# Inverse square roots in VectorE's small operations: one step of third order and one of second order in place of three steps of second order, in a decoder trunk of mixed heads

## The chip, the cores and the metric

The kernel runs on one core of a Trainium2 chip, in one launch. The metric is device microseconds of the core, the median of several executions. Of the core's engines, TensorE (PE) multiplies matrices, VectorE (DVE) and ScalarE (ACT) work element by element, GpSimd (POOL) prepares some tables and sums, and SyncE (SP) starts the transfers (DMA). Every engine works through a queue of its own, strictly in order, and waits at an instruction whose operands are not there yet.

## The reference, cut to what matters

One layer of a decoder trunk over 2048 tokens of width 1024, in float32. What matters here is where an inverse square root is taken:

```python
def rms_norm(x):
    return x * lax.rsqrt(jnp.mean(x * x, axis=-1, keepdims=True) + EPS)      # EPS = 1e-6

h = rms_norm(x) * (1 + sc1) + sh1
# h @ w_in, split into heads of three kinds of token mixers, each head 64 wide:
o_r = rms_norm(retention(...)) * silu(rg)     # 4 heads, fixed decay
o_h = rms_norm(hgrn2(...)) * silu(hg)         # 8 heads, gated decay
o_a = rms_norm(gla(...)) * silu(ag)           # 4 heads, gated decay
x = x + g1 * ((concat(o_r, o_h, o_a) * head_gain) @ w_out)
h = rms_norm(x) * (1 + sc2) + sh2
x = x + g2 * conv_ffn(h)                      # up (1024 to 2 x 2816), conv of 3 taps, silu gate, down
out = rms_norm(x) * final_gain
```

## The kernel before, in words

**Tiles and stages.** Tokens lie on the free axis in blocks of 512 (TB, four blocks), features on the 128 partitions. Every float32 product with a weight is made as three matmuls of rounded high and low halves (`split3`, L252 to L256: L254, L255, L256). So each operand needs its high half (a copy or activation on ScalarE) and its low half, the difference (on VectorE).

The program has these stages. `startup` (to about 60 us) loads the first block, takes its norm and begins the first projections. The token mixer goes block by block (to about 1240 us); within a block the units follow ORDER (L36): h0, h1, g, h2, h3, r0, r1, where an h or r unit is two heads and g is the four GLA heads. Then the MLP, by a scheme of seven products over halves (up and down stages, twice, to about 2480 us), and `last_product` with the final norm.

**A gated unit** (`gated`, L638 on) works through levels of a tree within chunks. At each level TensorE multiplies scores (`lvh` in PSUM, L664), VectorE scales queries and keys for the next level (L672 `qbh`, L674 `kh`) and puts the scores into the attention matrix (L683). TensorE's next level needs L672 and L674.

**A post** (`post`, L565 to L576) follows each unit's attention output `o` (128 tokens by 4 chunks by 2 heads of 64): squares on ScalarE, their sums over each head on VectorE (L571, `oms`, 128 x 8), the mean with EPS (L572), the inverse root `ors` (`newton`), then two products of 128 x 512: by the root (L575) and by the gate (L576). TensorE then transposes `o` (L582, `oT`), ScalarE and VectorE make its two halves (L585, L586), and the output projection uses them (`y`). There are 32 posts, eight to a block, since the GLA unit has two. A retention unit has its state updates (`S`, L892 and L894) and masks (L906) in the same queue.

**The other norms.** `rstd` (L330 to L351) takes the sums of squares of a block from TensorE and the root of 128 x 4, and TensorE spreads it again (`bc`, L347). Its input norm gives `xn` (L365), then `ha_k` for the eight k slices, high half on ScalarE (L369), low half on VectorE (L372). `startup` has such a norm (L431 to L439). `last_product` has two of 128 x 2 (L1456 to L1467, `msn`, `rsn`, `bcn`).

**The root.** `newton(x, y, n)` begins from an integer guess (L155, the bits of x times -0.5 plus a constant), and makes three Newton steps of three operations each: a = -0.5 y y (L158), a = a x (L159), y = (a + 1.5) y (L160). With the operation that makes the mean (L341, L433, L572 or L1460) that is 11 small operations, each on the result of the one before. It is called 45 times: once in `startup`, 10 times through `rstd`, 32 times in posts, twice in `last_product`.

**What sets the order.** TensorE's order is written by hand: steps are put on a `Clock` of due times, and the matmuls stand in the order in which the steps come due. In `startup` the orders of VectorE, ScalarE and SyncE are written by hand as well. After it a scheduler places the instructions of VectorE, ScalarE and SyncE, by when operands are ready in its own reckoning and by priorities: `tc.high_priority` with an offset puts work ahead (HOT 600, CHAIN 400). The roots in `rstd` have CHAIN, those in `last_product` HOT, those in `post` none; L672, L674 and L683 have CHAIN, the addition to the residual (L989) HOT.

Of the kernel before, what the change touches and what calls it, by code (L numbers as in the profile page):

```python
# [15 lines left out]
ALU = mybir.AluOpType  # L16
# [3 lines left out]
D = 1024  # L20
# [4 lines left out]
NCH = TB // P  # L25
# [5 lines left out]
EPS = 1e-6  # L31
# [73 lines left out]
def trunk(ctx, tc, xT, vecs, cvec, cst, rope, msk, wada, win, walow, wgla, wout, wup, wdown, out):  # L105
# [36 lines left out]
    V, S, G, T = nc.vector, nc.scalar, nc.gpsimd, nc.tensor  # L142
# [7 lines left out]
    ones = c_all[:, C_ONE:C_ONE + 1]  # L150
    nc.sync.dma_start(c_all[:], cst)

    def newton(x, y, n):

        V.tensor_scalar(y[:].bitcast(I32), x[:].bitcast(I32), -0.5, MAGIC, op0=ALU.mult, op1=ALU.add)  # L155
        a = small("nw", n)
        for _ in range(3):
            V.scalar_tensor_tensor(a[:], y[:], -0.5, y[:], op0=ALU.mult, op1=ALU.mult)  # L158
            V.tensor_tensor(a[:], a[:], x[:], op=ALU.mult)  # L159
            V.scalar_tensor_tensor(y[:], a[:], 1.5, y[:], op0=ALU.add, op1=ALU.mult)  # L160


    oml = p1.tile([P, 4], F32, tag="oml", name="oml")
# [5 lines left out]
    r = small("lbr", 4)  # L169
# [160 lines left out]
    def rstd(acc, name, bc, then, bank=None, gap=4.5):  # L330

        bank = bank or late_ps

        def first():
            p = bank("ss" + name)
            for c in range(NCH):
                T.transpose(p[:, c * P:(c + 1) * P], acc[:, c * P:(c + 1) * P], ident)
            x, r = small("ms" + name, NCH), small("rs" + name, NCH)
            with tc.high_priority(offset=CHAIN):
                V.tensor_reduce(x[:], p[:].rearrange("p (c d) -> p c d", c=NCH), axis=mybir.AxisListType.X, op=ALU.add)  # L340
                V.tensor_scalar(x[:], x[:], 1.0 / D, EPS, op0=ALU.mult, op1=ALU.add)  # L341
                newton(x, r, NCH)
            clock.at(gap, lambda: second(r))

        def second(r):
            p = bank("bc" + name)
            for c in range(NCH):  # L347
                T.transpose(p[:, c * P:(c + 1) * P], r[:, c:c + 1].to_broadcast([P, P]), ident)
            S.copy(bc, p[:])
            then()  # L350
        return first  # L351
# [37 lines left out]
    def startup():  # L389


        x, W, pending = [], {}, []
# [36 lines left out]
        ps = late_ps("ssn1_0")  # L429
        for c in range(NCH):  # L430
            T.matmul(ps[:, c:c + 1], acc[:, c * P:(c + 1) * P], ones, start=True, stop=True)  # L431
        ms, r = small("msn1_0", NCH), small("rsn1_0", NCH)
        V.tensor_scalar(ms[:], ps[:, 0:NCH], 1.0 / D, EPS, op0=ALU.mult, op1=ALU.add)  # L433
        newton(ms, r, NCH)
        cast("f")
        bc = bc1[0] = new_bc1(0)
        ps = late_ps("bcn1_0")
# [127 lines left out]
    def post(o, sg, name):  # L565

        o8 = o[:].rearrange("p c (h e) -> p (c h) e", e=64)
        sq = late("osq" + name)
        S.activation(sq[:], o[:].rearrange("p c e -> p (c e)"), AF.Square)
        ms = small("oms" + name)  # L570
        V.tensor_reduce(ms[:], sq[:].rearrange("p (a e) -> p a e", e=64), axis=mybir.AxisListType.X, op=ALU.add)  # L571
        V.tensor_scalar(ms[:], ms[:], 1.0 / 64, EPS, op0=ALU.mult, op1=ALU.add)  # L572
        rs = small("ors" + name)
        newton(ms, rs, 8)
        V.tensor_tensor(o8, o8, rs[:].unsqueeze(2).to_broadcast([P, 8, 64]), op=ALU.mult)  # L575
        V.tensor_tensor(o[:], o[:], sg[:], op=ALU.mult)  # L576

# [842 lines left out]
    def last_product(s, y, acc):  # L1420


        ops = last_operands(s)
        n = TB // 2

        def run(banks, ps, cols, cost):
            for k, (A, B) in enumerate(ops):
                for p, bank in zip(ps, banks):
                    sl = slice(p * P, (p + 1) * P)
                    split3(bank, [a[:, sl] for a in A], [x[:, cols] for x in B], k == 0, k == len(ops) - 1)  # L1430
                    adv(3 * cost)

        left = {}

        def add(bank, p, cols):
            with tc.high_priority(offset=HOT):
                V.scalar_tensor_tensor(y[1, p][:, cols], bank, G2[:, p:p + 1], y[1, p][:, cols], op0=ALU.mult,
                                       op1=ALU.add)
                if p < 3:
                    sumsq(acc, y[1, p], p, f"n3_{s}_1_", sl=cols, first=False)  # L1440
                else:
                    left[cols.start] = late(f"sqn3_{cols.start}")
                    S.activation(left[cols.start][:, cols], y[1, p][:, cols], AF.Square)
                gain(p, cols)

        def gain(m, cols):
            S.activation(y[1, m][:, cols], y[1, m][:, cols], AF.Copy, scale=vec[:, V_FG + m:V_FG + m + 1])

        def norm(t, banks):
            cols = slice(t * n, (t + 1) * n)  # L1450

            def first():
                p = banks(f"ssn3_{s}_1_{t}")
                for c in range(2):
                    for src in (acc, left[t * n]):
                        T.matmul(p[:, c:c + 1], src[:, t * n + c * P:t * n + (c + 1) * P], ones, start=src is acc,  # L1456
                                 stop=src is not acc)
                x, r = small(f"msn3_{t}", 2), small(f"rsn3_{t}", 2)
                with tc.high_priority(offset=HOT):
                    V.tensor_scalar(x[:], p[:, 0:2], 1.0 / D, EPS, op0=ALU.mult, op1=ALU.add)  # L1460
                    newton(x, r, 2)
                clock.at(4.0, lambda: second(r))

            def second(r):
                p = banks(f"bcn3_{s}_1_{t}")
                for c in range(2):
                    T.transpose(p[:, c * P:(c + 1) * P], r[:, c:c + 1].to_broadcast([P, P]), ident)  # L1467
                for i in range(KD // 2):
                    src = y["pair", i][:].rearrange("p (a n) -> p a n", a=2)[:, :, cols]
                    V.tensor_tensor(src, src, p[:, 0:n].unsqueeze(1).to_broadcast([P, 2, n]), op=ALU.mult)  # L1470
                    nc.sync.dma_start(out[2 * s + 1, :, 2 * i:2 * i + 2, cols], src)
                if t == 1:
                    done.add(("n3", 2 * s + 1))
            return first
        for m in range(4, KD):
            gain(m, slice(0, TB))
        whole = slice(0, TB)
        banks = [lev_ps(f"dL{p}") for p in range(2)]
        run([b[:] for b in banks], (0, 1), whole, M512)
        for p, b in enumerate(banks):  # L1480
            add(b[:], p, whole)
        for t, (one, bank) in enumerate(((late_ps, lev_ps), (acc_ps, late_ps))):
            cols = slice(t * n, (t + 1) * n)
            banks = [one(f"dL{t}_{p}") for p in range(2)]
            for p, b in enumerate(banks):
                run([b[:, 0:n]], (2 + p,), cols, M256)
                add(b[:, 0:n], 2 + p, cols)
            clock.at(2.6, norm(t, bank))
# [175 lines left out]
```

## Time and profile before

| | |
|---|---|
| median of 3 runs | 2523.25 us (2519.96 to 2526.4) |
| the profiled execution | 2519.96 us, its span 2518.2 us |
| PE busy | 2449.9 us, 97% |
| DVE busy | 1973.8 us, 78%, 3610 instructions |
| ACT busy | 1171.2 us, 47% |
| granted TensorE clock, mean | 0.993 |

The span goes from the first to the last instruction of the profiled execution. A row of the timeline reads: start, duration, engine, line, operation, output <- inputs, shapes, count, and in brackets how long the engine stood idle before it and what released it. A row of a list of waits reads: engine, waiting line <- releasing engine and line: us in total, times, longest. "L160" is line 160 of the kernel before.

### The profile page before, as it was taken

What the parts mean: (1) busy time and instruction counts of PE and PEld (TensorE: products, weight loads), DVE (VectorE), ACT (ScalarE), POOL (GpSimd) and SP (SyncE); (2) the same over time, 40 slices, a digit from 0 to 9 for tenths busy, and PEclk for the clock granted to TensorE, in tenths of its full rate; (3) what the DMA queues carried; (4) which work ended last, traced back from release to release, by engine and by line L of the source; (5) the groups of instructions that cost most, each with busy time, mean ns of one, the idle gap of its engine ahead of it and who ended that gap; (6) DMA issues with size and microseconds to landing.
All of it is one profiled execution on the core that took longest, in us unless ns stands there. A gap on an engine that the chain in (4) does not pass through costs nothing.

```text
span 2518.2 us, 35181 instructions
## 1 busy us (share of the span) xinstructions
PE 2449.9 (97%) x12173; PEld 2059.6 (82%) x12173; DVE 1973.8 (78%) x3610; ACT 1171.2 (47%) x1992; POOL 147.8 (6%) x278
## 2 busy tenths in 40 slices
PE   5999999999999999999999999999999999999998
PEld 4888878888888888888788888888878888888887
DVE  7987888878688785877698888787778877778565
ACT  4343434434444444434454544555445554555452
POOL 1000000000000000000000000000001100010000
PEclk9999999999999999999999999999999999999998
DMA  8853459865689647885554444587665444448663
GB/s 307 305 166 135 162 184 333 290 218 169 223 285 328 210 158 257 308 303 180 188 193 158 160 151 149 166 283 244 210 208 187 151 141 148 151 133 275 208 195 121
DMA packets 232499, 525.12 MB, mean 209 GB/s; under 512 B 24928, under 2 KB 28032, under 8 KB 232320
## 3 DMA queue, kind: packets, MB, share of 16 engines
q1 hardware_dynamic: 229120, 512.38, 61.1%
q0 software_dynamic: 3200, 10.49, 1.1%
q8 instruction: 96, 1.57, 0.3%
q14 instruction: 83, 0.68, 0.1%
HBM read 397.46 MB, written 125.30 MB: 208 GB/s over the span
## 4 chain that ended last, share of the span: by engine, by line
PE 47%; DVE 1%; DMA 1%; issue 1%; ACT 1%; DVEq 0%; POOL 0%; ACTq 0%; POOLq 0%
PE X L254 6%; PE X L255 6%; PE X L256 6%; PE dX L255 3%; PE dX L254 3%; PE dX L256 3%; PE Z L255 3%; PE Z L256 3%; PE Z L254 3%; PE dY L255 2%; PE dY L256 2%; PE dY L254 2%; PE Y L255 1%; PE Y L256 1%; PE Y L254 1%; DMA s<-sumsu 1%
## 5 line engine op out<-in xcount | busy, mean ns | idle before, releaser
L254 PE MATMUL X<-B,A 128*128 128x512 f32 x572 | 225.1, 393 | 4.4 <-ACT u L1358 2.3
L255 PE MATMUL X<-B,A 128*128 128x512 f32 x572 | 224.1, 392 | 0.0
L256 PE MATMUL X<-B,A 128*128 128x512 f32 x572 | 224.1, 392 | 0.0
L1058 DVE TENSOR_TENSOR dA<-rd,dA 128x512 fp32r<-128x512 f32 x154 | 106.1, 689 | 84.2 <-ACT dA L1057 83.9
L1057 ACT CAST dA<-rd 128x512 fp32r<-128x512 f32 x154 | 95.5, 620 | 131.1 <-PE dY L256 44.4
L1058 DVE TENSOR_TENSOR A<-s,A 128x512 fp32r<-128x512 f32 x176 | 120.7, 687 | 37.5 <-ACT A L1057 37.0
L1057 ACT CAST A<-s 128x512 fp32r<-128x512 f32 x176 | 108.5, 618 | 66.2 <-PE Z L256 45.2
L256 PE MATMUL dX<-dB,dA 128*128 128x512 f32 x352 | 137.0, 389 | 0.0
L255 PE MATMUL dX<-dB,dA 128*128 128x512 f32 x352 | 137.0, 389 | 0.0
L254 PE MATMUL dX<-dB,dA 128*128 128x512 f32 x352 | 137.0, 389 | 0.0
L254 PEld LDWEIGHTS X<-B,A 128*128 128x128 f32 x572 | 108.2, 189 | 29.2 <-ACT u L1358 4.5
L256 PEld LDWEIGHTS X<-B,A 128*128 128x128 f32 x572 | 108.2, 189 | 22.6
L255 PEld LDWEIGHTS X<-B,A 128*128 128x128 f32 x572 | 108.2, 189 | 22.2
L255 PE MATMUL Z<-B,A 128*128 128x512 f32 x308 | 119.9, 389 | 0.0
L254 PE MATMUL Z<-B,A 128*128 128x512 f32 x308 | 119.9, 389 | 0.0
L256 PE MATMUL Z<-B,A 128*128 128x512 f32 x308 | 119.9, 389 | 0.0
L1058 DVE TENSOR_TENSOR dB<-rb,dB 128x512 fp32r<-128x512 f32 x154 | 105.6, 687 | 9.7 <-ACT dB L1057 9.6
L1058 DVE TENSOR_TENSOR A<-r,A 128x512 fp32r<-128x512 f32 x130 | 89.4, 688 | 29.6 <-ACT A L1057 29.3
L664 PEld LDWEIGHTS lvh<-qbh,kh 128*128 128x128 f32 x768 | 100.6, 192 | 14.2 <-issue 6.4
L1057 ACT CAST A<-r 128x512 fp32r<-128x512 f32 x130 | 81.0, 623 | 62.4 <-PE Z L256 59.9
L664 PE MATMUL lvh<-qbh,kh 128*128 128x128 f32 x768 | 102.6, 277 | 5.0 <-DVE kh L674 3.8
L254 PE MATMUL psqkvgr<-hqkvgr,ha 128*128 128x512 f32 x256 | 106.2, 415 | 0.0
(479 smaller groups left out, 6993.4 us busy)
## 6 DMA issues: line engine op xcount, KB each, us to landing
gs<-yv SPq DMA_DIRECT2D x154, 256.0 KB, 3.0
rb<-gs SPq DMA_DIRECT2D x154, 256.0 KB, 3.9
r<-wup SPq DMA_DIRECT2D x140, 256.0 KB, 3.4
s<-sumsu SPq DMA_DIRECT2D x136, 256.0 KB, 3.0
wada<-wada SPq DMA_DIRECT2D x48, 512.0 KB, 6.1
rd<-sumsd SPq DMA_DIRECT2D x88, 256.0 KB, 3.8
rd<-wdown SPq DMA_DIRECT2D x66, 256.0 KB, 3.9
x<-xT SPq DMA_DIRECT2D x64, 256.0 KB, 5.9
```

The lines of the kernel that those rows point to most:

```text
L254: T.matmul(ps, lhs[0], rhs[0], start=first, stop=False, skip_group_check=more)
L255: T.matmul(ps, lhs[0], rhs[1], start=False, stop=False, skip_group_check=more)
L256: T.matmul(ps, lhs[1], rhs[0], start=False, stop=last, skip_group_check=more)
L664: T.matmul(ps[:, c * P:(c + 1) * P].rearrange("p (h n s) -> p h n s", h=2, s=s), kq[:, c * P:(c + 1) * P], rhs, start=True, stop=True)
L1057: S.copy(hi, src)
L1058: V.tensor_tensor(lo, src, hi, op=ALU.subtract)
```

## The change

The mean's operation moves into `newton`, which now takes what the mean is made of, and scales it by 1/2.25. The integer guess is made of the scaled mean. The first step is of third order, with four operations: a = -0.5 y y, a = a x, a = (a + 5/3) a, y = (a + 1.25) y. Its polynomial is two thirds of the usual third-order step, so that y leaves it with the factor of 1.5 of the scaled mean taken out again. The second is a Newton step with -1.125 in place of -0.5, since x is still scaled. That is 9 small operations instead of 11.

```diff
@@ -150,14 +150,17 @@
-    def newton(x, y, n):
-
+    def newton(x, y, n, mean, eps=EPS):
+
+        V.tensor_scalar(x[:], mean[0], mean[1] / 2.25, eps / 2.25, op0=ALU.mult, op1=ALU.add)
         V.tensor_scalar(y[:].bitcast(I32), x[:].bitcast(I32), -0.5, MAGIC, op0=ALU.mult, op1=ALU.add)
         a = small("nw", n)
-        for _ in range(3):
-            V.scalar_tensor_tensor(a[:], y[:], -0.5, y[:], op0=ALU.mult, op1=ALU.mult)
+        for step in (lambda: V.scalar_tensor_tensor(a[:], a[:], 5.0 / 3, a[:], op0=ALU.add, op1=ALU.mult), None):
+            V.scalar_tensor_tensor(a[:], y[:], -0.5 if step else -1.125, y[:], op0=ALU.mult, op1=ALU.mult)
             V.tensor_tensor(a[:], a[:], x[:], op=ALU.mult)
-            V.scalar_tensor_tensor(y[:], a[:], 1.5, y[:], op0=ALU.add, op1=ALU.mult)
+            if step:
+                step()
+            V.scalar_tensor_tensor(y[:], a[:], 1.25 if step else 1.5, y[:], op0=ALU.add, op1=ALU.mult)
@@ -338,8 +341,7 @@
-                V.tensor_scalar(x[:], x[:], 1.0 / D, EPS, op0=ALU.mult, op1=ALU.add)
-                newton(x, r, NCH)
+                newton(x, r, NCH, (x[:], 1.0 / D))
@@ -430,8 +432,7 @@
-        V.tensor_scalar(ms[:], ps[:, 0:NCH], 1.0 / D, EPS, op0=ALU.mult, op1=ALU.add)
-        newton(ms, r, NCH)
+        newton(ms, r, NCH, (ps[:, 0:NCH], 1.0 / D))
@@ -569,9 +570,8 @@
-        V.tensor_scalar(ms[:], ms[:], 1.0 / 64, EPS, op0=ALU.mult, op1=ALU.add)
-        newton(ms, rs, 8)
+        newton(ms, rs, 8, (ms[:], 1.0 / 64))
@@ -1457,8 +1457,7 @@
-                    V.tensor_scalar(x[:], p[:, 0:2], 1.0 / D, EPS, op0=ALU.mult, op1=ALU.add)
-                    newton(x, r, 2)
+                    newton(x, r, 2, (p[:, 0:2], 1.0 / D))
```

VectorE's program has 90 instructions fewer. TensorE's and GpSimd's orders are the same; ScalarE's and SyncE's have the same instructions, some in another order. In VectorE's, many instructions of the token mixer stand in another place. Three places follow, VectorE each time. A number behind a name counts units and blocks where it is small (`ha_5` is slice 5 of the next block's input, `orsh_3_0` the root of the fourth h unit) and is otherwise the allocator's own. Between the edit in `newton` and the one in `post` a line stands one to three further down after than before (L247 is L250, L365 is L367, L372 is L374, L571 is L572); from L575 on the numbers are the same again. The root's L158, L159, L160 before are L159, L160, L163 after, where L158 is the new third-order operation.

The first head unit of block 0, at its post. Before:

```order
L158 SCALAR_TENSOR_TENSOR nw<-orsh_0_0_1214 128x8
L683 COPY_PREDICATED ath_1_0_1241<-m_all,lvh_1_4_1293 128x128x4
L159 TENSOR_TENSOR nw<-nw,omsh_0_0_1211 128x8
L616 TENSOR_TENSOR yg_1145<-qg_1132,kg_989 128x512
L247 TENSOR_TENSOR lhfh_2_1443<-rhfh_2_1444,hhfh_2_1442 128x1024
L160 SCALAR_TENSOR_TENSOR orsh_0_0_1214<-nw,orsh_0_0_1214 128x8
L672 TENSOR_TENSOR qbh_1_823<-qbh_1_823,eh_1_721 128x64x8
L575 TENSOR_TENSOR oh_0_0_1195<-oh_0_0_1195,orsh_0_0_1214 128x512
L674 TENSOR_TENSOR kh_1_719<-kh_1_719,eh_1_721 128x32x8
L576 TENSOR_TENSOR oh_0_0_1195<-oh_0_0_1195,sgh_0_712 128x512
L683 COPY_PREDICATED ath_1_0_1241<-m_all,lvh_1_8_1324 128x64x8
```

After:

```order
L163 SCALAR_TENSOR_TENSOR orsh_0_0_1211<-nw,orsh_0_0_1211 128x8
L683 COPY_PREDICATED ath_1_0_1237<-m_all,lvh_1_4_1289 128x128x4
L575 TENSOR_TENSOR oh_0_0_1193<-oh_0_0_1193,orsh_0_0_1211 128x512
L250 TENSOR_TENSOR lhfh_2_1439<-rhfh_2_1440,hhfh_2_1438 128x1024
L576 TENSOR_TENSOR oh_0_0_1193<-oh_0_0_1193,sgh_0_710 128x512
L672 TENSOR_TENSOR qbh_1_821<-qbh_1_821,eh_1_719 128x64x8
L674 TENSOR_TENSOR kh_1_717<-kh_1_717,eh_1_719 128x32x8
L683 COPY_PREDICATED ath_1_0_1237<-m_all,lvh_1_8_1320 128x64x8
L616 TENSOR_TENSOR yg_1143<-qg_1130,kg_987 128x512
```

The products by the root and by the gate (L575, L576) stood behind L616, a weight split (L247) and L672, with L674 between the two. Now the first of them stands right behind L683, with the weight split (now L250) between the two; L616, L672 and L674 went behind both.

The end of block 0, where the next block's input slices `ha_4` to `ha_7` are made while the post of the fourth h unit (`omsh_3_0`, `orsh_3_0`) and the first retention state (`S`, L892, L894) are in the same queue. Before, first:

```order
L372 SCALAR_TENSOR_TENSOR ha_4_2685<-xn_4_2682,mod,ha_4_2685 128x512
L372 SCALAR_TENSOR_TENSOR ha_6_2697<-xn_6_2694,mod,ha_6_2697 128x512
L571 TENSOR_REDUCE omsh_3_0_2947<-osqh_3_0_2945 128x8
L892 COPY S_112<-ur_0_2979 64x64
L572 TENSOR_SCALAR omsh_3_0_2947<-omsh_3_0_2947 128x8
```

and eleven rows further on:

```order
L894 SCALAR_TENSOR_TENSOR S_112<-S_112,c_all,ur_0_2979 64x64
L159 TENSOR_TENSOR nw<-nw,omsh_3_0_2947 128x8
L894 SCALAR_TENSOR_TENSOR S_112<-S_112,c_all,ur_0_2979 64x64
L160 SCALAR_TENSOR_TENSOR orsh_3_0_2950<-nw,orsh_3_0_2950 128x8
L372 SCALAR_TENSOR_TENSOR ha_5_2691<-xn_5_2688,mod,ha_5_2691 128x512
L372 SCALAR_TENSOR_TENSOR ha_7_2703<-xn_7_2700,mod,ha_7_2703 128x512
L158 SCALAR_TENSOR_TENSOR nw<-orsh_3_0_2950 128x8
```

After:

```order
L374 SCALAR_TENSOR_TENSOR ha_4_2671<-xn_4_2668,mod,ha_4_2671 128x512
L374 SCALAR_TENSOR_TENSOR ha_5_2677<-xn_5_2674,mod,ha_5_2677 128x512
L374 SCALAR_TENSOR_TENSOR ha_6_2683<-xn_6_2680,mod,ha_6_2683 128x512
L572 TENSOR_REDUCE omsh_3_0_2933<-osqh_3_0_2931 128x8
L892 COPY S_112<-ur_0_2963 64x64
L155 TENSOR_SCALAR omsh_3_0_2933<-omsh_3_0_2933 128x8
L892 COPY S_112<-ur_0_2963 64x64
```

and eight rows further on:

```order
L894 SCALAR_TENSOR_TENSOR S_112<-S_112,c_all,ur_0_2963 64x64
L163 SCALAR_TENSOR_TENSOR orsh_3_0_2935<-nw,orsh_3_0_2935 128x8
L894 SCALAR_TENSOR_TENSOR S_112<-S_112,c_all,ur_0_2963 64x64
L374 SCALAR_TENSOR_TENSOR ha_7_2689<-xn_7_2686,mod,ha_7_2689 128x512
L159 SCALAR_TENSOR_TENSOR nw<-orsh_3_0_2935 128x8
```

The low half of `ha_5` stood with that of `ha_7`, behind the second step of the root, and now stands between those of `ha_4` and `ha_6`, ahead of the sums of squares of the post; `ha_7` stands after the first step.

The end of block 3, at the post of the first retention unit (`or_0`), with the masks of the second (`atr_1`, L906), a residual addition (L989) and the low halves of an input of the MLP (`lB_6_1`, `lB_6_2`, L1058). Before:

```order
L159 TENSOR_TENSOR nw<-nw,omsr_0_11247 128x8
L1058 TENSOR_TENSOR lB_6_2_11435<-hm_6_2_11432,hB_6_2_11434 128x512
L160 SCALAR_TENSOR_TENSOR orsr_0_11250<-nw,orsr_0_11250 128x8
L906 TENSOR_TENSOR atr_1_11328<-scr_1_1_11333,c_all 128x512
L575 TENSOR_TENSOR or_0_11243<-or_0_11243,orsr_0_11250 128x512
L989 SCALAR_TENSOR_TENSOR x_3_6_11304<-y_0_7_11321,mod,x_3_6_11304 128x512
L576 TENSOR_TENSOR or_0_11243<-or_0_11243,sgr_0_10395 128x512
L586 SCALAR_TENSOR_TENSOR oTr_0_11365<-oTr_0_11360,vec,oTr_0_11365 128x512
```

After:

```order
L1058 TENSOR_TENSOR lB_6_1_11351<-hm_6_1_11348,hB_6_1_11350 128x512
L163 SCALAR_TENSOR_TENSOR orsr_0_11175<-nw,orsr_0_11175 128x8
L906 TENSOR_TENSOR atr_1_11252<-scr_1_0_11253,c_all 128x512
L575 TENSOR_TENSOR or_0_11169<-or_0_11169,orsr_0_11175 128x512
L906 TENSOR_TENSOR atr_1_11252<-scr_1_1_11257,c_all 128x512
L576 TENSOR_TENSOR or_0_11169<-or_0_11169,sgr_0_10325 128x512
L989 SCALAR_TENSOR_TENSOR x_3_6_11228<-y_0_7_11245,mod,x_3_6_11228 128x512
L1058 TENSOR_TENSOR lB_6_2_11357<-hm_6_2_11354,hB_6_2_11356 128x512
L586 SCALAR_TENSOR_TENSOR oTr_0_11289<-oTr_0_11284,vec,oTr_0_11289 128x512
```

L989 stood between the two products and `lB_6_2` ahead of both; both now stand behind the second product, and one L906 went in between the two.

## The prediction, made blind

> **What bounds the kernel now.** I read the page first (busy shares), then the busy time by stage, then TensorE's list of waits, and last the timeline around each wait that names a root. First the page's line of engines, and the row of the MLP's up stage from the busy times by stage (columns: the stretch and its length, PE, PEld, DVE, ACT and POOL busy with their counts, granted clock, DMA share, GB/s).
>
> ```profile
> PE 2449.9 (97%) x12173; PEld 2059.6 (82%) x12173; DVE 1973.8 (78%) x3610; ACT 1171.2 (47%) x1992; POOL 147.8 (6%) x278
> ...
> 1240.00:1650.00 410.00, 408.49 (x1799) 337.25 (x1798) 350.36 (x453) 215.21 (x321) 30.98 (x85) 1.00 0.49 161
> ```
>
> TensorE is the bound: it is idle for 2518.2 - 2449.9 = 68 us in all, and in the MLP's up stage for 410.00 - 408.49 = 1.5 us. VectorE is busy for 78%, but its busy time is not the path. A shorter root is worth something only where TensorE waits for it, and those places are in the next list (TensorE's waits: total us, times, longest).
>
> ```profile
> PE bcn L1467 <- DVE rsn L160: 4.6, 2, 2.7
> ...
> PE lvh L664 <- DVE kh L674: 3.8, 2, 3.4
> ...
> PE pshfh L255 <- DVE ha L372: 2.6, 1, 2.6
> ...
> PE oTh L582 <- DVE oh L576: 1.4, 2, 0.7
> ```
>
> The first row ends in a root itself (two of them, in the last stage); a third such wait, at the start, comes in the next fence. The last row ends in the product behind a head's root (L576). The two in the middle end in other work that stood behind a root in VectorE's queue. All other roots have no such wait, or one that is shown below; their saving stays in VectorE's slack.
>
> **Part 1: two operations fewer in a root that TensorE waits for.** The removed operations are of the kind of these rows (count, busy, mean ns), and the root at the start shows their spacing:
>
> ```profile
> L158 DVE SCALAR_TENSOR_TENSOR nw<-orsh 128x8 f32<-128x8 f32 x48 | 7.9, 164 | 0.4
> ...
> 18.57 0.16 DVE L159 TENSOR_TENSOR nw<-nw,msn 128x4 f32<-128x4 f32 x1
> 18.77 0.16 DVE L160 SCALAR_TENSOR_TENSOR rsn<-nw,rsn 128x4 f32<-128x4 f32 x1
> ...
> 18.98 1.11 PE L439 MATMUL bcn<-c_all,rsn 128*128 128x128 f32 x4 [2.23 <-DVE rsn L160]
> ```
>
> One operation is busy for 0.16 us, but the next one of a dependent chain starts 18.77 - 18.57 = 0.20 us after it. The four forms that the new root uses are of the same size and kinds as the old ones, so I price them alike. Two operations fewer on the path are 2 x 0.195 = **0.39 us** at the start, where VectorE goes from the root straight into the work that TensorE needs next. At the end it is the same twice (the 4.6 us of the list). The last root stands alone in the queue. In the one before it three operations follow the last large one of the queue, from here on:
>
> ```profile
> 2503.75 0.16 DVE L158 SCALAR_TENSOR_TENSOR nw<-rsn 128x2 f32<-128x2 f32 x1
> ```
>
> In the new order only one does. Sum 2 x 0.39 = **0.78 us**. Nothing late takes its place: what follows (the scaling and the last stores) waits for these two transposes.
>
> [...] The row of 164 ns agrees with the duration, not with the worth: on the path the step is 0.20, and between independent operations only 0.08 (next fence, 124.85 to 124.93).
>
> **Part 2: what the shorter root moves.** The order of VectorE changes in many places, because a root that needs fewer turns lets the scheduler place the products behind it earlier. First place, the first head unit of block 0 (the order before and after is shown above):
>
> ```profile
> 123.12 0.68 DVE L616 TENSOR_TENSOR yg<-qg,kg 128x512 f32<-128x512 f32 x1
> 123.72 1.21 DVE L247 TENSOR_TENSOR lhfh<-rhfh,hhfh 128x1024 fp32r<-128x1024 f32 x1
> 124.85 0.15 DVE L160 SCALAR_TENSOR_TENSOR orsh<-nw,orsh 128x8 f32<-128x8 f32 x1
> 124.93 0.68 DVE L672 TENSOR_TENSOR qbh<-qbh,eh 128x512 f32<-128x512 f32 x1
> 125.53 0.68 DVE L575 TENSOR_TENSOR oh<-oh,orsh 128x512 f32<-128x512 f32 x1
> 126.14 0.41 DVE L674 TENSOR_TENSOR kh<-kh,eh 128x256 f32<-128x256 f32 x1
> 126.47 0.68 DVE L576 TENSOR_TENSOR oh<-oh,sgh 128x512 f32<-128x512 f32 x1
> ...
> 127.29 0.63 PE L582 MATMUL oTh<-c_all,oh 128*128 128x128 f32 x4 [0.72 <-DVE oh L576]
> ...
> 128.46 1.06 PE L664 MATMUL lvh<-qbh,kh 128*128 128x128 f32 x8
> ...
> 166.87 0.63 PE L582 MATMUL oTh<-c_all,oh 128*128 128x128 f32 x4 [0.67 <-DVE oh L576]
> ```
>
> L616, L672 and L674 go behind L576. By their steps that is 0.60 + 0.60 + 0.33 = 1.53 us, and two small operations at 0.08 come to 0.16. L576 would end 1.7 us earlier, more than the 0.72 that TensorE waits. In exchange L672 starts about 0.5 us later and L674 about where it was, and the level's matmul at 128.46 comes 128.46 - 126.55 = 1.9 us after L674's end, so it has room. The same move is made in the next unit (row of 166.87). Sum 0.72 + 0.67 = **1.39 us**.
>
> Second place, the end of block 0:
>
> ```profile
> 295.21 1.41 DVE L372 SCALAR_TENSOR_TENSOR ha<-xn,mod,ha 128x512 fp32r<-128x512 f32 x2
> ...
> 301.16 1.41 DVE L372 SCALAR_TENSOR_TENSOR ha<-xn,mod,ha 128x512 fp32r<-128x512 f32 x2
> ...
> 301.96 0.50 PE L255 MATMUL pshfh<-ha,hhfh 128*128 128x512 f32 x1 [2.59 <-DVE ha L372]
> ```
>
> TensorE waits at its k = 5 for the low half of `ha_5`, the first of the two L372 at 301.16. It stands behind a root and the state updates between its operations. In the new order it stands directly behind `ha_4`, so it would be done at about 295.21 + 2 x 0.67 = 296.6, five us before it is needed. What is late next is `ha_7`: about 302, when TensorE is through with k = 5, its scores and k = 6. I take the whole **2.59 us**; the bounds are 0 (if `ha_7` takes the wait over) and 2.59.
>
> Then two retention roots lie in a stretch that VectorE works through almost without a pause until TensorE's long wait at 338:
>
> ```profile
> 337.93 2.04 PE L664 MATMUL lvh<-qbh,kh 128*128 128x128 f32 x8 [3.38 <-DVE kh L674]
> ```
>
> Four operations fewer at 0.20 are **0.80 us** out of these 3.38; at the 0.08 of interleaved ones they would be 0.32. I take the upper value, since the last operations of both roots stand without a filler.
>
> Third place, the end of block 3:
>
> ```profile
> 1190.89 0.68 DVE L575 TENSOR_TENSOR or<-or,orsr 128x512 f32<-128x512 f32 x1
> ...
> 1192.15 0.68 DVE L576 TENSOR_TENSOR or<-or,sgr 128x512 f32<-128x512 f32 x1
> ...
> 1192.98 0.63 PE L582 MATMUL oTr<-c_all,or 128*128 128x128 f32 x4 [1.21 <-DVE or L576]
> ...
> 1195.17 0.79 PE L596 MATMUL or<-S,qnr 128*128 128x128 f32 x2 [1.56 <-DVE oTr L586]
> ...
> 1237.98 0.50 PE L254 MATMUL X<-B,A 128*128 128x512 f32 x1 [1.99 <-ACT u L1354]
> ```
>
> In the new order L989 and L1058's `lB_6_2` go from ahead of L576 to behind it. The turns of two such operations, L575 and L989, take 1192.15 - 1190.89 = 1.26 us here. L576 would end about that much earlier, so the wait of 1.21 goes. But up to the MLP's first product TensorE also waits for transfers and for ScalarE (1.99 at 1237.98), and a gain can stand there. I take half of 1.21, **0.60 us**, with 0 and 1.21 as ends.
>
> Sum: 0.39 + 1.39 + 2.59 + 0.80 + 0.60 + 0.78 = **6.55 us**. The profiled execution took 2519.96 us (span 2518.2 and 1.76 around it) and would take 2513.4. It was the fastest of the three runs shown; against their median of 2523.25 the forecast is **2516.7 us**, 0.26% less. About 0.3%, or 7.6 us, is what a measurement of this kernel can tell from no change, so I call this case "same". With the unsure terms at their ends it gains 2.6 to 7.2 us.
>
> **Rivals.**
>
> *The clock goes up as well.* Two rows of busy times by stretch, the number ahead of the last two being the granted clock:
>
> ```profile
> 301.00:304.00 3.00, 2.04 (x9) 1.80 (x10) 2.83 (x9) 0.03 (x1) 0.00 (x0) 1.00 0.00 0
> ...
> 1195.20:1204.00 8.80, 8.80 (x33) 8.03 (x34) 2.48 (x9) 1.38 (x2) 0.18 (x3) 0.50 0.26 104
> ```
>
> After the waits of 1.21 and 1.56 us TensorE had half its clock for 8.8 us (1195.20 to 1204.00), which costs 4.4 us of its time; after the single wait of 2.59 at 302 the clock stayed at 1.00. If one wait of 1.56 is left, the half clock may not come. Then all 1.21 count (0.61 more) and 4.4 on top: -11.6 us, 2511.7. Against it stands that at other places a shorter idle stretch might meet the throttle instead, and that these rows do not tell when it strikes. [...]
>
> *The gains are taken back.* What TensorE gains before 1237 (5.77 us of the sum) is waited away where it next stands for a transfer or ScalarE, the 1.99 at 1237.98 growing by as much. Left are the two roots at the end, -0.8 us, 2522.5; if half is taken back, about -4. For it speaks that the list of waits has such places; against it that TensorE has only some 1.5 us of idle time in the whole stage behind it, so the transfers there have room.
>
> *Slower: the products of the heads stand in front of the levels.* A post has L575 and L576 (0.60 each), and the new order puts them ahead of level work in the queue of a strictly ordered engine. There are 32 posts. If each delays a level's L672 by the 0.5 us worked out for the first, and the level's matmul has less room than that, the price is 32 x 0.5 = 16 us, less 6.55: +9.5, 2532.7. It decides where the room is under 0.5 us; the one worked out above has 1.9, and before the change the level waits for kh come to 3.8 us in two places of the whole program.
>
> That the change does not do what it says is excluded: the order of VectorE has 90 small operations fewer, two in each of 45 roots.
>
> **How the numbers follow.** Forecast 0.40, the clock as well 0.34, taken back 0.17, slower 0.09. Faster by over 0.3%: the clock case and a little of the forecast whose terms all come at their upper ends, 0.36. Same: the rest of the forecast and the case taken back, 0.55. Slower 0.09. The range goes from the clock case with two us below it (a wait of the list that goes unasked) to the case taken back with two and a half above: 2510 to 2525. It leaves out the slower case and the outer ends.
>
> **What would show it.** In the changed profile: no wait for L372 at about 302 (if one of similar size stands at k = 7, that term fails); no waits before the transposes near 127 and 167; the wait at 338 shorter by 0.8; the waits of the list's first row 3.8 instead of 4.6; the granted clock around 1195 to 1204, which tells the forecast from the first rival; and the wait near 1238, which tells it from the second. New waits of the level matmuls (L664) for their operands in many places would make the prediction wrong.

## The result, and the profile after

The changed kernel takes 2512.49 us (median of 10 executions, 2505.55 to 2518.38) against 2523.56 us of the kernel before (10 executions, the three shown above among them). The ratio is 0.9958, with a 95% interval of 0.9945 to 0.9970: 11 us, or 0.42%, faster. The forecast was 2516.7, the first rival (the clock goes up as well) 2511.7.

The page's line of engines after:

```profile
PE 2442.4 (98%) x12173; PEld 2056.2 (82%) x12173; DVE 1962.9 (78%) x3520; ACT 1171.2 (47%) x1992; POOL 146.4 (6%) x278
```

The span of this execution is 2503.8 us, 14.4 less than before. TensorE's share of it splits in two. Its idle time fell from 68.3 to 2503.8 - 2442.4 = 61.4 us, so 6.9 us of waits went. Its busy time fell by 2449.9 - 2442.4 = 7.5 us, although it runs the same 12173 matmuls: that is the clock, 0.993 on average in the profile of before and 0.996 here. The profiled execution is the fastest of the ten, so its 14.4 us flatter the change.

TensorE's list of waits after, two of its rows:

```profile
PE lvh L664 <- DVE kh L674: 4.0, 3, 3.4
...
PE bcn L1466 <- DVE rsn L163: 3.8, 2, 2.3
```

The waits for the two last roots went from 4.6 to 3.8 us, as predicted. The rows of before for `oTh` on `oh` (1.4) and for `pshfh` on `ha` at the end of block 0 (2.6) are gone; the level's wait (3.8 before) is still there.

The timeline of TensorE at the places of the prediction, in the order of the program:

```profile
18.30 0.69 PE L440 MATMUL bcn<-c_all,rsn 128*128 128x128 f32 x2 [1.84 <-DVE rsn L163]
...
125.32 0.60 PE L582 MATMUL oTh<-c_all,oh 128*128 128x128 f32 x4
...
164.11 0.60 PE L582 MATMUL oTh<-c_all,oh 128*128 128x128 f32 x4
...
296.70 0.39 PE L258 MATMUL pshfh<-ha,hhfh 128*128 128x512 f32 x1
...
327.43 1.15 PE L664 MATMUL lvh<-qbh,kh 128*128 128x128 f32 x8 [0.38 <-DVE doth L645]
...
331.95 1.85 PE L664 MATMUL lvh<-qbh,kh 128*128 128x128 f32 x8 [3.38 <-DVE kh L674]
...
1182.57 0.60 PE L582 MATMUL oTr<-c_all,or 128*128 128x128 f32 x4
...
1184.73 0.49 PE L596 MATMUL or<-S,qnr 128*128 128x128 f32 x2 [1.56 <-DVE oTr L586]
...
1222.59 0.50 PE L257 MATMUL X<-B,A 128*128 128x512 f32 x1 [1.48 <-ACT u L1354]
...
1231.40 0.51 PE L257 MATMUL X<-B,A 128*128 128x512 f32 x1 [2.55 <-ACT u L1358]
...
2490.36 0.43 PE L1466 MATMUL bcn<-c_all,rsn 128*128 128x128 f32 x2 [1.48 <-DVE rsn L163]
...
2496.75 0.48 PE L1466 MATMUL bcn<-c_all,rsn 128*128 128x128 f32 x1 [2.29 <-DVE rsn L163]
```

A matmul without a bracket did not wait. The four waits in front of the transposes near 127, 167 and 1193 and in front of the matmul at 302 are gone. The wait of 1.56 us at the end of block 3 is still there. Two waits at the MLP's beginning read 1.48 and 2.55 us; before they were 1.99 and 0.77. The level's wait of 3.38 us has not moved, but the one ahead of it, 0.38 us here, was longer before:

```profile
333.40 1.15 PE L664 MATMUL lvh<-qbh,kh 128*128 128x128 f32 x8 [1.00 <-DVE doth L645]
```

VectorE at the first of those places, and the three low halves at the end of block 0:

```profile
121.36 0.72 DVE L683 COPY_PREDICATED ath<-m_all,lvh 128x512 f32<-128x512 uint32 x1
121.98 0.68 DVE L575 TENSOR_TENSOR oh<-oh,orsh 128x512 f32<-128x512 f32 x1
...
123.70 0.69 DVE L576 TENSOR_TENSOR oh<-oh,sgh 128x512 f32<-128x512 f32 x1
124.30 0.69 DVE L672 TENSOR_TENSOR qbh<-qbh,eh 128x512 f32<-128x512 f32 x1
...
292.90 2.07 DVE L374 SCALAR_TENSOR_TENSOR ha<-xn,mod,ha 128x512 fp32r<-128x512 f32 x3
```

L576 starts at 123.70 instead of 126.47. VectorE was 1.07 us ahead by then (its L683 stood at 122.43 and stands at 121.36), so the new order made L576 1.7 us earlier, the figure that was worked out. The low halves of slices 4 to 6 are one group that ends at 294.97. The one of slice 5, the middle one, ends a step of 0.66 us earlier, at about 294.3, so 2.4 us before the matmul of k = 5. The one of slice 7 stands alone, from 298.92 to 299.66, and its matmul starts at 299.82.

Last, the clock at the end of block 3 (busy times by stretch, the clock third from the end):

```profile
1184.80:1193.60 8.80, 8.80 (x51) 7.74 (x52) 4.42 (x14) 3.22 (x4) 1.43 (x6) 1.00 0.67 230
```

The 8.8 us at half clock that followed these waits before are gone here: in as long a time TensorE does 51 matmuls instead of 33.

### The profile page after: what moved, and what is told of

It is laid out like the page before. It is cut to its first block, busy times and chain, and to the rows that moved or that the text cites. A ratio compares the mean times of both kernels' runs of the same rounds, so it can differ in the third digit from the quotient of the medians.

```text
span 2503.8 us, 35090 instructions
## 1 busy us (share of the span) xinstructions
PE 2442.4 (98%) x12173; PEld 2056.2 (82%) x12173; DVE 1962.9 (78%) x3520; ACT 1171.2 (47%) x1992; POOL 146.4 (6%) x278
## 4 chain that ended last, share of the span: by engine, by line
PE 48%; DVE 1%; DMA 1%; issue 1%; ACT 0%; DVEq 0%; POOL 0%; ACTq 0%; POOLq 0%
PE X L257 6%; PE X L258 6%; PE X L259 6%; PE dX L257 3%; PE dX L259 3%; PE dX L258 3%; PE Z L257 3%; PE Z L258 3%; PE Z L259 3%; PE dY L257 2%; PE dY L259 2%; PE dY L258 2%; PE Y L257 1%; PE Y L258 1%; PE Y L259 1%
## 5 line engine op out<-in xcount | busy, mean ns | idle before, releaser
L1058 DVE TENSOR_TENSOR dA<-rd,dA 128x512 fp32r<-128x512 f32 x154 | 106.1, 690 | 87.1 <-ACT dA L1057 86.9
L1058 DVE TENSOR_TENSOR A<-s,A 128x512 fp32r<-128x512 f32 x176 | 120.7, 686 | 36.3 <-ACT A L1057 35.8
L1058 DVE TENSOR_TENSOR A<-r,A 128x512 fp32r<-128x512 f32 x130 | 89.4, 688 | 30.4 <-ACT A L1057 30.2
L1058 DVE TENSOR_TENSOR dB<-rb,dB 128x512 fp32r<-128x512 f32 x154 | 105.7, 687 | 8.9 <-ACT dB L1057 8.9
```

Of the source, the lines that this page charges most:

```text
L1058: V.tensor_tensor(lo, src, hi, op=ALU.subtract)
```

## The experiments

The ratio sets each run against the kernel before on the same chip. Beside it I use a second reading. Every execution carries its mean granted clock c, so that span x (1 - c) is, at most, what the reduced clock cost it, and span x c is the rest. Over 76 executions of before, taken beside the runs e1 to e12 on two chips, c is 0.9927 on average and the rest 2502.6 us, and every row is set against these. The executions of before in the first comparison have no clock on record, but for the profiled one. Half-clock stretches fall differently from execution to execution (at the end of block 3 for 10.2 us in the first profile of before, for 3.4 in that of e1), so the rest tells more finely what the waits did. Standard errors of the rest are 0.7 to 1.1 us (2.0 for the new root in all posts).

| kernel | ratio, 95% interval | mean clock | rest against before, us |
|---|---|---|---|
| the change, first 10 executions | 0.9958 (0.9945 to 0.9970) | 0.9945 | -5.8 |
| the change again (e8) | 0.9957 (0.9941 to 0.9973) | 0.9935 | -8.4 |
| before again (e1) | 0.9996 (0.9986 to 1.0007) | 0.9927 | -0.5 |
| old roots, posts ahead (e2) | 1.0011 (0.9998 to 1.0025) | 0.9915 | 0.0 |
| new roots and fillers (e3) | 0.9980 (0.9970 to 0.9991) | 0.9926 | -5.7 |
| all 32 posts (e4) | 0.9958 (0.9946 to 0.9970) | 0.9936 | -7.3 |
| last two posts (e5) | 0.9985 (0.9973 to 0.9998) | 0.9931 | -2.1 |
| the other 30 posts (e6) | 0.9975 (0.9965 to 0.9985) | 0.9931 | -5.1 |
| start and last norms (e7) | 0.9994 (0.9981 to 1.0007) | 0.9924 | -1.2 |
| first block's eight posts (e9) | 0.9971 (0.9960 to 0.9982) | 0.9935 | -4.5 |
| ten block norms (e10) | 0.9998 (0.9988 to 1.0008) | 0.9923 | -1.6 |
| one third-order step only (e11) | 0.9938 (0.9922 to 0.9953) | 0.9943 | -10.9 |
| roots of 13 operations (e12) | 1.0049 (1.0037 to 1.0062) | 0.9916 | +10.3 |

The theory: the change is worth the waits that a root, or something behind it in VectorE's queue, ends. The first rival: every removed VectorE operation is worth its time, 10.9 us over 90 = 0.12 us. The second: the gain is the clock.

**Before once more (e1)**, without an edit.

> The kernel before once more, under a name of its own, so that each of its executions shows its granted clock. Theory (the new order of VectorE takes waits of TensorE away): ratio 1.000 within 0.2%; a granted clock between 0.990 and 0.996 that changes from execution to execution, and times that go down by about 2.5 us for each 0.001 of it. Rival (the clock: before always meets a half clock near 1195 that the changed kernel always misses): the clock stays at 0.992 to 0.994 in every execution, below all of the changed kernel's.

The ratio is 1 within the interval. The clock of the single executions runs from 0.991 to 0.994, so half clocks come and go without any change. The clock alone doesn't tell the two kernels apart by execution either: the changed kernel's first ten run from 0.992 to 0.996. In the profile of e1 TensorE has half its clock behind the wait for `ha_5` at the end of block 0, where the first profile of before kept the full clock. The row of the wait, and the busy times behind it:

```profile
303.23 0.50 PE L255 MATMUL pshfh<-ha,hhfh 128*128 128x512 f32 x1 [2.68 <-DVE ha L372]
```

```profile
304.20:307.70 3.50, 3.50 (x10) 2.74 (x10) 2.79 (x5) 0.00 (x0) 0.56 (x2) 0.51 0.00 0
```

**Old roots, the posts' VectorE work ahead (e2).** The body of `post` from L570 on is put under a priority:

```diff
+        with tc.high_priority(offset=CHAIN):
             ms = small("oms" + name)
             ...
             V.tensor_tensor(o[:], o[:], sg[:], op=ALU.mult)
```

> Roots of 11 operations as before; only the priority of the VectorE work of the 32 posts is raised by 400, which moves it ahead in the first unit's post and brings the low half of slice 5 forward at the end of block 0, as in the changed kernel, but leaves the end of block 3 as it was. Theory of the order: the waits near 127, 167 and 302 go without any operation removed, -4 to -5 us (ratio 0.998). Rival (VectorE's time: each removed operation is worth its 0.12 us to TensorE): no operation is removed, so 0 us. Third view (levels delayed by posts that go ahead): +5 us or more.

As for the first block the theory held: TensorE's waits near 127, 167 and 302 are gone without a removed operation, and it is 4.5 us ahead at 302, 0.5 of them from the start already. But the run as a whole is not faster, since other waits have come. Two rows of its list of waits:

```profile
PE og L597 <- DVE S L714: 4.7, 2, 3.3
...
PE bcn L348 <- DVE rsn L160: 2.8, 2, 2.1
```

The second is a block norm's root. It shares its turns with a post's root in the kernel before too, without a wait. Here it ends 1.15 us earlier than there, but TensorE comes over 3 us earlier and waits 2.10 for it, so a part of the gain is waited away. The first row is shown by the timelines at that place. The kernel before comes first (SPq is SyncE's queue; L942 starts the two loads of a weight that L948 and the three operations behind it add up, and L948 needs the second of them):

```profile
1064.69 1.54 SPq L942 DMA_DIRECT2D wsu<-wup  x2
...
1073.14 0.69 DVE L948 TENSOR_TENSOR wsu<-wsu 128x512 f32<-128x512 f32 x1 [2.47 <-DMA wsu<-wup]
...
1077.91 3.67 DVE L713 SCALAR_TENSOR_TENSOR S<-S,eg,ug 32x64 f32<-32x64 f32 x12 [1.89 <-PE ug L703]
```

Then e2, where these lines are L943, L949 and L714:

```profile
1066.48 0.33 SPq L943 DMA_DIRECT2D wsu<-wup  x1
...
1070.18 0.32 SPq L310 DMA_DIRECT2D lvgh<-keptt_3l  x1
1073.27 0.38 SPq L302 DMA_DIRECT2D rqkvgr<-win  x1
1073.70 0.47 SPq L943 DMA_DIRECT2D wsu<-wup  x1
...
1081.76 0.69 DVE L949 TENSOR_TENSOR wsu<-wsu 128x512 f32<-128x512 f32 x1 [10.22 <-DMA wsu<-wup]
1082.37 2.71 DVE L714 SCALAR_TENSOR_TENSOR S<-S,eg,ug 32x64 f32<-32x64 f32 x9
...
1084.92 0.46 PE L597 MATMUL og<-S,qbg 128*128 128x128 f32 x2 [3.27 <-DVE S L714]
```

The busy times of e2 behind that wait:

```profile
1086.30:1093.00 6.70, 6.70 (x24) 5.83 (x24) 6.14 (x18) 2.26 (x3) 1.04 (x2) 0.50 0.31 116
```

A sum over the MLP's weights stands ahead of the state updates of the GLA unit in both kernels. What changed is SyncE's order: both loads of the sum are started together before, and in e2 the second stands behind two other loads, so that it starts some 8 us later. The sum (L949) waits 10.22 us for it, the states wait behind the sum, TensorE waits 3.27 us for them and has half its clock for 6.7 us after it. So an earlier post is no gain by itself. What else moves decides, in SyncE's queue too, and my expectation of -4 to -5 us was wrong.

**New roots and two idle operations (e3).** In the loop of the new `newton`:

```diff
+            d = small("nd", n)
+            V.tensor_tensor(d[:], x[:], x[:], op=ALU.mult)
```

> The changed kernel's roots of 9 operations, with two more small multiplications per root into a tile that nobody reads, so that VectorE has as many instructions as before. Theory of the order: the products still come early, most of the gain stays, -6 to -9 us (ratio 0.997), with the waits near 127, 167 and 302 gone; at the start and the end up to 0.4 us per root is lost. Rival (VectorE's time): the instructions are back, 0 us.

The product `d` is read by nobody. VectorE has as many instructions as before, and the kernel still gains: ratio 0.9980, the rest -5.7 us. That speaks against the price per operation. It does not speak against a price per busy time, because VectorE's busy time is 1966.8 us in this profile, 7.0 below before, although the count is the same. The kernel gains less than expected, and the profile shows one reason: the same sum (here L950) waits for its second load, which starts at 1070.39 behind the same two others, 7 us after the first at 1063.17.

```profile
1078.44 0.69 DVE L950 TENSOR_TENSOR wsu<-wsu 128x512 f32<-128x512 f32 x1 [10.21 <-DMA wsu<-wup]
...
1081.60 0.46 PE L598 MATMUL og<-S,qbg 128*128 128x128 f32 x2 [3.50 <-DVE S L715]
```

In the changed kernel the two loads are started together, as before (at 1058.08), and TensorE does not wait there.

**The new root in all posts alone (e4):** the new `newton` is called in `post` only.

> The new root in the 32 posts alone; start, block norms and last norms keep 11 operations. Theory of the order: all but the 0.39 at the start and 0.78 at the end, -9 to -10 us (ratio 0.9962). Rival (VectorE's time): 64 of 90 operations, -7.7 us. Rival of the sum as predicted: -6.55 + 1.17 = -5.4 us, the rest being the clock.

The posts carry nearly all: ratio 0.9958, the rest -7.3 us. The rival's -7.7 us, a ratio of 0.9969, lies inside the interval as well, so this run does not tell the two apart.

**The last two posts, and the other thirty (e5, e6).** `post` counts its calls:

```diff
+        posts.append(name)
+        if len(posts) > 30:          # e6: len(posts) <= 30
+            newton3(ms, rs, 8, (ms[:], 1.0 / 64))
+        else:
             V.tensor_scalar(ms[:], ms[:], 1.0 / 64, EPS, op0=ALU.mult, op1=ALU.add)
             newton(ms, rs, 8)
```

> The new root in two posts alone, those of the last block's two retention units; the order of VectorE changes only at the end of block 3, there as in the changed kernel. The wait of 1.21 us near 1193 goes in any case. Theory A (the half clock near 1195 came of that wait together with the one of 1.56 behind it): the mean granted clock rises from 0.993 to about 0.995 and the time falls by 4 to 6 us (ratio 0.998). Theory B (the half clock comes by chance and with all waits): the clock stays at 0.993, -1.2 us at most (ratio 0.9995), less if the MLP's waits take it back.

> The new root in the other 30 posts; the end of block 3, the start, the block norms and the last norms stay as before. Theory A (of the run before this one): the clock stays at 0.993, and the time falls by the waits alone, -5 to -6 us (ratio 0.9978). Theory B: the clock rises as far as in the changed kernel, to 0.994 to 0.995, and the time falls by 8 to 9 us (ratio 0.9966).

TensorE's timelines at the end of block 3, first of e5, then of e6, each with its clock behind it:

```profile
1195.60 0.60 PE L600 MATMUL oTr<-c_all,or 128*128 128x128 f32 x4
```

```profile
1196.10:1204.90 8.80, 7.24 (x45) 6.36 (x44) 4.49 (x14) 2.37 (x3) 2.30 (x7) 1.00 0.73 236
```

```profile
1189.63 0.63 PE L600 MATMUL oTr<-c_all,or 128*128 128x128 f32 x4 [1.22 <-DVE or L594]
```

```profile
1191.20:1198.00 6.80, 6.18 (x27) 5.99 (x28) 1.26 (x2) 0.03 (x1) 0.18 (x3) 0.51 0.46 166
```

The pair divides the posts at this place. With the two last posts alone the wait of 1.2 us is gone, with the other thirty it stays. In these two profiles the half clock follows the wait. But the mean clock of e5 is 0.9931, not 0.995, and that of e6 is the same. So theory A, which had this one place carry the clock's gain, does not hold. B's rise of the clock to 0.994 or 0.995 did not come in e6 either; its bound of -1.2 us for e5 (ratio 0.9995) is not excluded, since the interval and the rest of -2.1 us, with a standard error of 0.9, leave room for it.

**The start and the last norms alone (e7):** the new `newton` is called in `startup` and `last_product` only.

> The new root at the start and in the two last norms alone, the three roots that TensorE waits for by themselves. By the sum of the prediction 0.39 + 0.78 = 1.17 us less (ratio 0.9995); in the profile the waits for the root at the start and the two at the end shorter by 0.39 each. Rival (what is gained at the start is lost again in a wait for a transfer): the 0.78 at the end alone.

TensorE's three waits for these roots:

```profile
18.49 0.90 PE L450 MATMUL bcn<-c_all,rsn 128*128 128x128 f32 x3 [1.84 <-DVE rsn L172]
...
2505.26 0.43 PE L1477 MATMUL bcn<-c_all,rsn 128*128 128x128 f32 x2 [1.48 <-DVE rsn L172]
...
2511.03 0.69 PE L1477 MATMUL bcn<-c_all,rsn 128*128 128x128 f32 x2 [2.29 <-DVE rsn L172]
```

Each is shorter by 0.39 or 0.40 us. The rest is -1.2 us; a gain of 0.05% is too small for the ratio to tell from none.

**The change once more (e8)**, without an edit.

> The changed kernel once more, beside the others on one chip, for more executions with their clocks: ratio 0.9958 again within 0.0012. Theory (half of the gain beyond the sum is the clock): mean clock 0.994 to 0.995 against 0.993 of before, and TensorE's idle time in the profile 6 to 8 us below that of before (68.3). Rival (the first profile was a lucky one): clock 0.993, ratio 0.9975.

The ratio repeats, and TensorE's idle time in the profile is 60.9 us, 7.4 below before, as expected. The clock, 0.9935, stayed under the expected 0.994 to 0.995, and half clock came at the end of block 3 in this profile although TensorE did not wait for `or`:

```profile
1183.99 0.60 PE L582 MATMUL oTr<-c_all,or 128*128 128x128 f32 x4
...
1186.15 0.49 PE L596 MATMUL or<-S,qnr 128*128 128x128 f32 x2 [1.56 <-DVE oTr L586]
```

```profile
1187.50:1194.30 6.80, 6.80 (x24) 5.93 (x24) 2.94 (x12) 1.67 (x2) 0.18 (x3) 0.50 0.39 142
```

**The first block's eight posts (e9)**, as e5 with `len(posts) <= 8`, **and the ten block norms (e10)**, the new `newton` in `rstd` only.

> The new root in the eight posts of the first block alone. By the prediction's terms these posts carry 1.39 (the waits near 127 and 167), 2.59 (near 302) and 0.80 (the wait near 338), 4.78 us together (ratio 0.9981), and the 22 posts behind them up to the last two are worth nothing: those 30 posts together measured 0.9975. Rival (every post is worth its share): 8 of 30, -1.7 us (ratio 0.9993).

> The new root in the ten block norms alone. By the prediction none of them has a wait that it ends: 0 us (ratio 1.000 within 0.0012). Rival (VectorE's time): 20 of 90 operations, -2.4 us (ratio 0.999).

The eight posts give a rest of -4.5 us where the prediction's three terms are 4.78; the other posts up to the thirtieth, by e6, add 0.6, which is within the errors of the two. The ratio, 0.9971, excludes the rival's 0.9993, and VectorE's busy time is only 2.3 us below that of before here, so a price per busy time doesn't explain it either. The wait near 127 and the one near 302 in e9:

```profile
126.25 0.60 PE L600 MATMUL oTh<-c_all,oh 128*128 128x128 f32 x4
```

```profile
297.94 0.39 PE L267 MATMUL pshfh<-ha,hhfh 128*128 128x512 f32 x1
```

Both waits are gone. The block norms change nothing by the ratio; their rest of -1.6 us is two standard errors and not claimed. The rival's 0.999 lies just inside the interval, so e10 doesn't exclude it.

**One step of third order only (e11).** The loop of the new `newton` runs once; the roots lack the last step's accuracy:

```diff
-        for step in (lambda: ..., None):
+        for step in (lambda: ...,):
```

> Beyond the change: the second step is left out as well, so the roots are those of one third-order step, 6 small operations in place of 9, 135 instructions fewer than in the changed kernel. Theory of the waits: the waits that a post could end are gone already; only the three roots that TensorE waits for give 0.6 us each, with 1 to 3 us of the rest, so 2.5 to 5 us below the changed kernel (ratio to before 0.994 to 0.995). Rival (VectorE's time): 135 more at 0.12 us, -16 us below the changed kernel (ratio 0.989). Third view (earlier products meet other work, as in the run with raised priority): slower than the changed kernel.

135 operations fewer than the change, and the ratio goes from 0.9958 to 0.9938, some 5 us. The price per operation asks for 16, a ratio of 0.989, outside the interval. At the start the wait is shorter by three steps of 0.20:

```profile
17.39 1.11 PE L440 MATMUL bcn<-c_all,rsn 128*128 128x128 f32 x4 [1.24 <-DVE rsn L163]
```

**Roots of 13 operations (e12).** In the old `newton`, in its first two steps:

```diff
+            if i < 2:
+                V.tensor_scalar(a[:], a[:], 1.0, 0.0, op0=ALU.mult, op1=ALU.add)
```

> The other way: the roots of before with two more small operations in the chain (a multiplication by one in the first two steps), 13 instead of 11. Theory of the waits, taken as a slope: the three roots that TensorE waits for cost 1.2 us more, and the posts' products come later by another turn or two, +4 to +10 us (ratio 1.002 to 1.004). Theory of the order as a lottery of places: between -3 and +3 us. Rival (VectorE's time): 90 operations more, +10.9 us (ratio 1.0043).

12 us slower, a little more than the theory's upper end and close to the price per operation, so the ratio does not part the two. TensorE's list of waits and timeline do:

```profile
PE oTh L584 <- DVE oh L578: 5.4, 4, 1.8
...
PE pshfh L257 <- DVE ha L374: 4.9, 1, 4.9
...
PE oTh L584 <- DVE or L917: 3.3, 2, 1.7
```

```profile
127.73 0.63 PE L584 MATMUL oTh<-c_all,oh 128*128 128x128 f32 x4 [1.81 <-DVE oh L578]
...
305.81 0.80 PE L257 MATMUL pshfh<-ha,hhfh 128*128 128x512 f32 x1 [4.95 <-DVE ha L374]
...
759.72 0.66 PE L584 MATMUL oTh<-c_all,oh 128*128 128x128 f32 x4 [0.90 <-DVE oh L578]
```

The waits that the change removed have grown instead (0.72 to 1.81, 2.59 to 4.95), and posts of later blocks, which made nobody wait before, have waits of their own.

## Why the prediction was right

The forecast's mechanism, a sum of waits that end, was right, and its size too: over the 16 executions of the changed kernel the rest is 6.8 us below that of before (standard error 0.7), against a sum of 6.55. The time came out 4.2 us below the point forecast, because the clock rose as well: c is 0.9941 against 0.9927 on average, so that the clock cost at most 14.8 us instead of 18.4, 3.6 less. That is the first rival, in part. By the prediction's own bound of 0.3% the outcome, 0.42%, is "faster", to which it gave 0.36, and not "same", to which it gave 0.55.

By terms:

- **Start, 0.39, and end, 0.78: right.** 2.23 to 1.84; 1.88 to 1.48 and 2.69 to 2.29. With these roots alone (e7) the rest fell by 1.2.
- **The first two posts, 1.39: right**, and by the mechanism named: L576 started 1.7 us earlier by the new order. The levels behind did not suffer.
- **The wait at 302, 2.59: right.** `ha_7`, named as next late, made nobody wait, but it ended only 0.16 us before its matmul started, so that the whole 2.59 came has some luck in it. The room of `ha_5` was 2.4 us, not the five that were worked out: those were counted from where the matmul stood after its wait, not from where it could have started.
- **The two retention roots, 0.80: right in size, wrong in place.** The wait at 338 stayed at 3.38. What went is at the level before it, 1.00 to 0.38 us, 0.62. Both waits hang on the same queue of VectorE. Once the first is shorter, TensorE comes to the second just as much earlier as VectorE does, so a head start shows at the first wait only.
  Counted between the same matmuls, TensorE's idle time fell by 1.3 us in the stretch that was 127 to 300 us before, and by 3.2 us in that of 300 to 345, in each of the five profiles with new roots in the first block's posts and nothing else moved there (the change twice, e4, e6, e9); the terms for them are 1.39 and 3.39.
- **The end of block 3, 0.60: probably too small.** The whole 1.21 went, and in e5 the two posts gave a rest of -2.1 (standard error 0.9). Whether the MLP's beginning took a part back, which was the reason for the halving, single profiles don't tell, since its two waits scatter: 1.99 and 0.77 us before, 2.19 and 2.70 in the second run of before, 1.48 and 2.55 after, 2.26 and 0.93 in e8. The rest of e5 speaks against it.
- **The clock, the first rival: partly right.** Its claim was that half clock may not come when one wait of 1.56 is left. The profile of before has it there for 10.2 us. Of the seven profiles with the wait of 1.2 us or its longer form kept at this place besides the first (e1, e2, e6, e7, e9, e10, e12), all have a half-clock stretch there, 3.4 or 6.8 us; of the six without it (the two of the change, e3, e4, e5, e11) two have none, one 3.4 us and three 6.8. So the wait's absence does not prevent half clock; that it makes it less frequent is likely, but fourteen profiles can't show it. e5 and e6 show that the rise of the mean clock is not this place's alone. A second place is probably the wait at 302: of the six profiles that keep it (before, e1, e5, e7, e10, e12) three have half clock there, 3.4 us in e1 and e7 and 6.8 in e12, and of the eight without it none. These are few as well. The prediction had only the one profile in which the full clock followed this wait. By the averages of these profiles, with half of a stretch as its cost, I estimate the two places at 1.4 and some 1 us of the 3.6. What carries the rest stays open.
- **The gains are taken back: wrong.** The rest kept all of them.
- **Slower by delayed levels: wrong for this order**, but the kind of harm is real. In e2 and e3 a different order of the same work brought a wait of 3.3 and 3.5 us and half clock behind it. The prediction looked for that harm in the levels; it sat at an operation ahead of what TensorE needed, whose transfer came to start some 7 to 8 us later.

In these traces the length of a wait does not tell by itself whether half clock follows. A wait of 2.59 us at 302 kept the full clock in the profile of before and one of 2.68 in e1 did not; a single wait of 1.56 at the end of block 3 kept it in the profile after, while e8 had half clock for 6.8 us behind the same one.

## What to carry to other kernels

Price a shorter operation on an engine that is not the bound by the waits that it ends, one by one with their rows, and look in the new order for what moved in front of or behind a waited-for operation; the count of removed instructions says little (135 more of them gave 5 us where the first 90 gave 11). Where two waits hang on one queue, count a head start once (here the first went from 1.00 to 0.38 us and the second stayed at 3.38). And look at the order of the transfers too: an operation that waits for one, ahead of work that the bound engine needs, cost nothing here while its load started early, and 3.27 us in e2 and 3.50 in e3 when the load came behind two others.

## What the runs showed of the hardware

Ahead of the last stage TensorE's half-clock stretches came in lengths of 3.4, 6.8 or 10.2 us in these traces, and two executions of the same kernel have them at different places: the two profiles of the kernel before have the same 24 us of it ahead of the last stage, but 10.2 and 3.4 us at the end of block 3. TensorE's busy time follows them: 2449.9 us with 24 us of half clock, 2442.4 with 10, so by about half of the difference. The idle time moves by itself as well, 68.3 and 75.8 us in those two profiles. These two executions took 2519.96 and 2527.25 us, so a difference of two single profiles says little below 10 us here, and the mean clock of many executions beside their times says what one of them cannot.
